# A decoder trunk whose norms apply the token scale after the matmuls, with the keys loaded during the mixers and one engine's one-hots made in two sweeps

## The chip, the cores and the metric

The kernel runs on one core of one Trainium2 chip. A core has five engines that run their own instruction queues and wait for one another through semaphores: PE (matmul; its weight loads are listed apart as PEld), DVE (vector), ACT (scalar), POOL (GpSimd) and SP (which here only issues DMAs). Each engine takes its instructions strictly in the order in which the program lists them, so an instruction that waits holds up all that stands behind it. The metric is the device time of one execution in microseconds (us); lower is better.

## The reference, cut to what matters

256 tokens of width 1024 pass through four residual steps: an attention and retention mixer, a PEER expert step, a short-convolution mixer, and a second PEER step. Before each step stands an RMS norm, and a last one stands at the end:

```python
def rmsnorm(x, g):
    y = xf * lax.rsqrt(jnp.mean(xf * xf, axis=-1, keepdims=True) + EPS)   # one scale per token
    return y * g                                                          # one gain per column

q  = (t @ w_q).reshape(n_tok, 8, 2, 128)            # PEER: queries, 8 heads x 2 halves
sc = einsum('thpd,hpnd->thpn', q, sub_keys)         # scores against 128 keys a half
s1, i1 = top_k(sc[:, :, 0], 16); s2, i2 = top_k(sc[:, :, 1], 16)
# the best 16 of all 256 sums s1+s2 name 16 of 16384 experts a head; softmax over them is the gate
hid = gelu(einsum('td,thkd->thk', t, u[eidx])); out = einsum('thk,thkd->td', gate * hid, v[eidx])

bg, cg, hx = split(xn @ w_in, 3)                    # short convolution
y = conv3(cg * hx);  out = (bg * y) @ w_out
```

The norm's scale is a number per token, its gain a number per column. A scale per token can be taken out of any product that contracts over the columns, and applied to the result.

## The kernel before, in words

The residual `h` lies in SBUF as two halves of 128 tokens by 1024 columns. A matmul with float32 accuracy is built of three: weights are split on the chip into a high part (a cast on ACT, L143) and a low part (a subtraction on DVE or POOL, L145), activations likewise, and high x high, high x low and low x short are added in PSUM. `Stream` loads 512 KB weight blocks in one fixed order into 8 buffers from SP's queue, and splits them a few ahead of their use (`ahead`, `next`).

`Norm` stands between the steps. The mixer's last loop (`v_phase`) ends with four quarters of the output (a half of the tokens by 512 columns); after each, DVE adds it to `h` (L293) and `norm.done(a, ...)` runs. `quarter` squares and sums on ACT (L349), takes the root there (L362), makes the reciprocal with one step of Newton's method on DVE (`rstd`, L368 to L373), multiplies `h` by the gain (L353), and puts the token scales on a diagonal matrix `dg`. `finish` turns `h` to columns by tokens with matmuls against `dg` (L380), which applies the scales on the way, runs 8 dummy matmuls (`busy`, L316), and writes the high, low and short parts of the result: `x2` and `Xb`. For PEER a float32 copy `XF` and a copy by tokens `XG` (96 tokens) are written too. `First`, the norm of the input, has its own form: `some` turns the raw half with the diagonal, and writes high and low parts column block by column block with the gain as a scale (L502 on ACT, L503 on DVE).

`even_mixer` runs 28 weight blocks into four PSUM accumulators, with a table of work to be put between the blocks (`steps`); `rope`, `evac` and others take results out of PSUM. `odd_mixer` runs three blocks a column block, with a short chain on ACT and DVE behind each.

`peer` has three stages. The **score stage**: 16 blocks of `wq`, each a tile of 24 matmuls (`u_tile`, L248 and L261), a copy of the result (L1098), the matmul with the keys (`scores`, L957) and a copy of that out of PSUM (L960). A `Pump` hands the search for the best 16 (L944 to L952) to DVE behind it, which goes on far into the next stage. The keys are loaded into `KO` by POOL at the start of `peer` (L935), after `KO`'s memory, which the mixer's tiles used, is free. The **dense u stage**: 128 blocks of `pu` for the 160 tokens that are not gathered, while 96 tokens have their experts' rows gathered by POOL's indirect DMAs (L837) and multiplied on DVE (L847). Here `onehots` (L1135, L1136) builds on ACT, per token, |iota - index| and then a relu of it, whose products on PE spread the gates over the experts. The **dense v stage** does the same with `pv`.

What sets the order is the program itself: every instruction is listed by hand, and nothing is reordered.

## Time and profile before

| | us |
|---|---|
| median of 3 runs | 1547.38 (1544.8 to 1550.67) |
| the profiled execution, its own time | 1543.23 |
| its span in the trace | 1541.5 |
| PE busy | 1484.1 (96%) |
| DVE busy | 1163.8 (75%) |
| ACT busy | 797.2 (52%) |
| POOL busy | 687.4 (45%) |
| bytes moved | 533.55 MB, a mean of 346 GB/s |

A row of the timeline holds the start in us from the span's start, the length in us, engine and line, the operation, the tile written and the tiles read, and in brackets the idle time before it and what ended it; rows of one line are merged (x16 is 16 instructions). A row of the windows holds the stretch, its length, then for PE, PEld, DVE, ACT and POOL the busy time and the number of instructions, the share of full speed at which PE's clock was granted, the share of the 16 DMA engines in use, and GB/s. Matmuls overlap, so a busy PE is not a PE at its best.

### The profile page before, as it was taken

The numbers are of one execution on the slowest core, as the hardware profiler recorded it, in microseconds if no ns is written. First come the engines' busy times: TensorE is split into PE (matmuls) and PEld (weight loads), VectorE is DVE, ScalarE is ACT, GpSimd is POOL, SyncE is SP. The second block draws the span as 40 slices with busy tenths as digits, with TensorE's granted clock in tenths as the row PEclk, the third lists the DMA queues.
The fourth block names the chain that finished last, engine by engine and source line by source line (L and its number), as shares of the span: only waits on it lengthen the run. The fifth ranks groups of instructions, "written<-read, shape, count | busy, mean of one in ns | idle before, by whom it ended". The sixth has DMA issues, their size and how long they took to land.

```text
span 1541.5 us, 30553 instructions
## 1 busy us (share of the span) xinstructions
PE 1484.1 (96%) x11183; PEld 1392.5 (90%) x11196; DVE 1163.8 (75%) x2514; ACT 797.2 (52%) x1974; POOL 687.4 (45%) x522
## 2 busy tenths in 40 slices
PE   8998999999999899999989989999999999999997
PEld 5666999999999899999989789999999998999996
DVE  3637999957888777777674569997688887777785
ACT  5555412158988244444554353212898954444454
POOL 6653645544654333333047365455455552333310
PEclk9999999999999999999999999999999999999998
DMA  8344889999999999999945477999999999999993
GB/s 316 145 150 165 326 333 408 382 407 406 408 409 408 395 395 406 391 407 403 367 163 194 158 262 293 404 404 370 408 409 408 408 405 394 407 399 400 407 393 130
DMA packets 146998, 533.55 MB, mean 346 GB/s; under 512 B 16928, under 2 KB 17056, under 8 KB 146848
## 3 DMA queue, kind: packets, MB, share of 16 engines
q1 hardware_dynamic: 71568, 258.87, 43.7%
q0 software_dynamic: 56704, 205.07, 34.0%
q10 hardware_dynamic: 18576, 67.64, 11.3%
q8 instruction: 89, 1.46, 0.4%
q14 instruction: 61, 0.50, 0.1%
HBM read 528.85 MB, written 1.05 MB: 344 GB/s over the span
## 4 chain that ended last, share of the span: by engine, by line
PE 41%; DMA 24%; DVE 24%; issue 5%; ACT 4%; POOL 2%; SPq 0%; DVEq 0%; ACTq 0%; POOLq 0%
DMA raw<-pv 10%; PE vo L1268 8%; PE vo L1272 8%; PE hid L1178 6%; DMA rows<-pun,ig 5%; DVE rows L847 4%; PE vo L1274 4%; PE hid L248 4%; DMA grow<-pv,ig 3%; DMA rows<-pv,ig 3%; DVE grow L847 2%; DMA grow<-pun,ig 2%; DVE hg L946 2%; DVE hg L952 2%; DVE hg L948 2%
## 5 line engine op out<-in xcount | busy, mean ns | idle before, releaser
L1178 PE MATMUL hid<-xf,raw 128*128 128x160 f32 x3648 | 520.6, 302 | 13.0 <-DVE hg L1212 7.0
L1178 PEld LDWEIGHTS hid<-xf,raw 128*128 128x128 f32 x3648 | 505.5, 192 | 14.7 <-DVE hg L1212 8.3
L1189 ACT CAST vhi<-raw 128x1024 fp32r<-128x1024 f32 x160 | 167.5, 1047 | 252.2 <-DMA raw<-pv 205.6
L1196 DVE TENSOR_TENSOR vlo<-raw,vhi 128x1024 bf16<-128x1024 f32 x160 | 195.8, 1224 | 119.7 <-ACT vhi L1189 117.9
L837 POOL DMA_INDIRECT rows<-pv,ig x128 | 154.3, 1206 | 260.0 <-DVE gacc L861 206.6
L145 POOL TENSOR_TENSOR lo<-raw,hi 128x1024 bf16<-128x1024 f32 x76 | 182.1, 2408 | 118.6 <-ACT hi L143 106.4
L1272 PE MATMUL vo<-hs,vhi 128*128 128x320 f32 x1280 | 229.1, 321 | 2.0 <-DVE hs L1249 1.7
L1268 PE MATMUL vo<-hg,raw 128*128 128x160 f32 x1536 | 228.9, 302 | 0.6 <-DVE hg L1212 0.6
L837 POOL DMA_INDIRECT rows<-pun,ig x128 | 156.3, 1221 | 135.5 <-DVE rows L847 88.9
L1268 PEld LDWEIGHTS vo<-hg,raw 128*128 128x128 f32 x1536 | 211.6, 190 | 1.1 <-DVE hg L1212 1.1
L1272 PEld LDWEIGHTS vo<-hs,vhi 128*128 128x128 f32 x1280 | 190.6, 188 | 4.9 <-DVE hs L1249 4.3
L847 DVE SCALAR_TENSOR_TENSOR rows<-rows,xg 128x1024 f32<-128x1024 f32 x128 | 155.0, 1220 | 27.4 <-DMA rows<-pun,ig 26.7
L861 DVE SCALAR_TENSOR_TENSOR gacc<-rows,ghid,gacc 128x1024 f32<-128x1024 f32 x124 | 158.7, 1280 | 14.2 <-DMA rows<-pv,ig 13.8
L1209 ACT ACTIVATE hg<-hid 128x160 f32<-128x160 f32 (+25 forms) x242 | 64.1, 269 | 192.7 <-PE hid L1178 188.3
L1136 ACT ACTIVATE ko<-ko,idxT 128x128 f32<-128x128 f32 x320 | 157.9, 493 | 10.6
L837 POOL DMA_INDIRECT grow<-pv,ig x64 | 78.3, 1224 | 121.6 <-DVE gacc L861 91.3
L1135 ACT ACTIVATE ko<-cst,idxT 128x128 f32<-128x128 f32 x320 | 124.1, 388 | 5.5 <-PE G L1145 5.5
L248 PE MATMUL hid<-x,hi 128*128 128x256 f32 x896 | 123.5, 291 | 0.5 <-ACT x L389 0.3
L1274 PE MATMUL vo<-hb,vlo 128*128 128x160 bf16 x1280 | 116.3, 234 | 0.0
L143 ACT CAST hi<-raw 128x1024 fp32r<-128x1024 f32 x100 | 104.1, 1051 | 20.3 <-issue 7.5
L248 PEld LDWEIGHTS hid<-x,hi 128*128 128x128 f32 x896 | 112.8, 195 | 1.4 <-ACT x L389 1.1
L837 POOL DMA_INDIRECT grow<-pun,ig x64 | 77.2, 1206 | 75.0 <-DVE grow L847 45.0
(235 smaller groups left out, 2020.3 us busy)
## 6 DMA issues: line engine op xcount, KB each, us to landing
raw<-pu SPq DMA_DIRECT2D x228, 512.0 KB, 7.6
raw<-pv SPq DMA_DIRECT2D x128, 512.0 KB, 8.3
raw<-pv ACTq DMA_DIRECT2D x128, 512.0 KB, 7.8
raw<-wq SPq DMA_DIRECT2D x32, 512.0 KB, 3.7
raw<-ew_in SPq DMA_DIRECT2D x28, 512.0 KB, 4.3
raw<-ow_in SPq DMA_DIRECT2D x24, 512.0 KB, 4.3
hg<-pu SPq DMA_DIRECT2D x22, 512.0 KB, 5.0
raw<-ew_out SPq DMA_DIRECT2D x8, 512.0 KB, 3.2
```

Of the source, the lines that this page charges most:

```text
L145: eng.tensor_tensor(lo, t, hi.bitcast(F32), OP.subtract)
L248: pe.matmul(ps[:, :S], hi[:, k * P:(k + 1) * P], A2[:, k, s_, :], start=k == 0 and s_ == 0, stop=False)
L837: gp.indirect_dma_start(self.row(s_), None, table, bass.IndirectOffsetOnAxis(IG[:, 0, s_ % STEPS:s_ % STEPS + 1].bitcast(U32), 0))
L847: v.scalar_tensor_tensor(r, r, 1.0, XG[:, q % 2, :], op0=OP.mult, op1=OP.mult, accum_out=w)
L861: v.scalar_tensor_tensor(self.acc[q], r, w, self.acc[q], op0=OP.mult, op1=OP.add)
L1136: act.activation(B[:, j], B[:, j], AF.Relu, bias=idxT[:, 2, t:t + 1], scale=idxT[:, 3, t:t + 1])
L1178: pe.matmul(ps[:, :TD], w[:, k * P:(k + 1) * P], XF[:, k, :], start=k == 0, stop=k == ND - 1)
L1189: act.copy(whi[j], raw)
L1196: v.tensor_tensor(wlo[j], raw, whi[j].bitcast(F32), OP.subtract)
L1268: pe.matmul(vo[b][:, :TD], w[:, b * P:(b + 1) * P], HG[:, i, :], stop=False, **m)
L1272: pe.matmul(vo[b][:, :2 * TD], hi[:, b * P:(b + 1) * P], hs, stop=i == NK - 1, **m)
L1274: pe.matmul(vo[b][:, :TD], lo[:, b * P:(b + 1) * P], hb, stop=i == NK - 1, **m)
```

## The change

Three things. **The norms.** `First` goes, and `Norm` is written anew. After each quarter the raw `h` is turned with plain transposes (`turn`), with no gain and no scale; `parts` writes the high and low parts with the gain as a scale per column, for all norms. The token scale is made later and applied where results leave PSUM: in `rope`, `evac`, `scores`, and in the odd mixer. Where it must lie along the free axis, `spread` makes it so on PE. `rows`, called in the score stage behind the first tile, writes `XF` and `XG`, which `finish` wrote before. The 8 dummy matmuls go; at the start 24 are left of 36. **The keys.** `KO` is now held for the whole kernel, and `load_keys` runs in the mixer before. **The one-hots.** The four first steps of a group come before the four second steps.

```diff
+    KO = pers.tile([P, NPAIR * NK], F32, tag="ko", name="ko")
...
+    class Norm(Sums):
...
+        def turn(self, a):
+            th, ch = a // 2, a % 2
+            if th == 0:
+                for j in range(2):
+                    self.ps[ch, j] = acc_tile(j, nm("xt")) if ch else side_tile(nm("xt"))
+            for k in range(4):
+                kk = ch * 4 + k
+                o = (k % 2 * 2 + th) * P
+                pe.transpose(self.ps[ch, k // 2][:, o:o + P], h[:, th, kk * P:(kk + 1) * P], ident)
+
+        def parts(self, ch):
+            x2 = xv["x2"]
+            for k in range(4):
+                kk = ch * 4 + k
+                ps = self.ps[ch, k // 2][:, k % 2 * S:(k % 2 + 1) * S]
+                gain = G[:, (3 + self.gi) * ND + kk:(3 + self.gi) * ND + kk + 1]
+                act.activation(x2[:, kk, 0, :], ps, AF.Copy, scale=gain)
+                v.scalar_tensor_tensor(x2[:, kk, 1, :], ps, gain, x2[:, kk, 0, :].bitcast(F32),
+                                       op0=OP.mult, op1=OP.subtract)
+                if k % 2:
+                    gp.tensor_copy(Xb[:, kk - 1:kk + 1, :], x2[:, kk - 1:kk + 1, 0, :].bitcast(F32))
+
+        def done(self, a, junk):
+            if a == 1:
+                self.turn(0)
+            if a < 3:
+                self.square(a, junk)
+            if a == 1:
+                self.mean0(0)
+                self.root(0)
+            if a == 2:
+                self.turn(1)
+                self.rstd(0)
+                self.mean0(1)
+            if a == 3:
+                new_x2()
+                self.turn(2)
+                self.parts(0)
+                self.turn(3)
+                self.square(a, junk)
+                self.parts(1)
+                self.root(1)
+                st.ahead(0)
+                self.rstd(1)
+
+        def first(self, junk):
+            new_x2()
+            for a in (0, 2, 1, 3):
+                self.turn(a)
+            self.parts(0)
+            st._split()
+            st._split()
+            self.parts(1)
+            for a in range(4):
+                self.square(a, junk)
+            for th in range(2):
+                self.mean0(th)
+                self.root(th)
+                self.rstd(th)
+            st.ahead(0)
+
+        def spread(self):
+            for th in range(2):
+                v.tensor_scalar(self.wb[:, th], ident, 0.0, self.scale(th), op0=OP.mult, op1=OP.add)
+            ps = side_tile(nm("rb"))
+            for th in range(2):
+                pe.matmul(ps[:, th * P:(th + 1) * P], self.wb[:, th], ident, start=True, stop=True)
+            return ps[:, :S]
+
+        def rows(self):
+            ps = self.spread()
+            x2 = xv["x2"]
+            v.tensor_tensor(XF, x2[:, :, 0, TG:].bitcast(F32), x2[:, :, 1, TG:].bitcast(F32), OP.add)
+            v.tensor_tensor(XF, XF, ps[:, None, TG:].to_broadcast([P, ND, TD]), OP.mult)
+            v.scalar_tensor_tensor(XG[:TG, 0, :], h[:TG, 0, :], self.scale(0)[:TG], XG[:TG, 1, :],
+                                   op0=OP.mult, op1=OP.mult)
+            act.copy(XG[:TG, 1, :], XG[:TG, 0, :])
+            for q in range(2):
+                gp.dma_start(XG[TG:, q, :], XG[q * SUB:(q + 1) * SUB, 0, :])
...
+    def load_keys(l):
+        for c in (slice(0, 4 * NK), slice(4 * NK, NPAIR * NK)):
+            gp.dma_start(KO[:, c], keys[l][:, c])
...
-                    v.tensor_tensor(a, a, co[:, None, :].to_broadcast([P, NH, HD]), OP.mult)
+                    times(a, a, co, HD)
...
-            at(0, rest)
+            at(14, lambda: load_keys(0))
...
                 ps = u_tile(xv["x2"], Xb, first=k == 0)
+                if k == 0:
+                    rb = before.spread()
+                    act.copy(rs[:, 0], rb)
+                    v.tensor_tensor(rs[:, 1], rb, rs[:, 0], OP.mult)
+                    load_keys(1)
                 cg = mp2.tile([P, S], F32, tag="cg", name=nm("cg"))
-                act.copy(cg, ps[:, :S])
+                v.tensor_tensor(cg, ps[:, :S], rs[:, 1], OP.mult)
...
                 v.tensor_tensor(z, ps[:, :S], y, OP.mult)
+                v.tensor_tensor(z, z, rs[:, 0], OP.mult)
...
-                    act.copy(sc(th, f), ps[:, th * NK:(th + 1) * NK])
+                    act.activation(sc(th, f), ps[:, th * NK:(th + 1) * NK], AF.Copy, scale=before.scale(th))
...
                 act.copy(qT[f % 2], ps[:, :S])
+                if f == 0:
+                    before.rows()
...
                     act.activation(B[:, j], iota, AF.Abs, bias=idxT[:, 1, t:t + 1], scale=-1.0)
+                for j in range(GT):
+                    t = g * GT + j
                     act.activation(B[:, j], B[:, j], AF.Relu, bias=idxT[:, 2, t:t + 1], scale=idxT[:, 3, t:t + 1])
...
-        busy(36)
-        norm.start(acc_tile(3, nm("junk")))
+        busy(24)
+        norms[0].first(acc_tile(3, nm("junk")))
```

In the last norm (`Final`) the two token factors are multiplied once in `rstd`, ahead of all four output pieces; before, they were two operands, and only the piece on ACT needed the product (L522).

More of the change, by code (lines that the diff above doesn't have):

```diff
@@ L403, in short @@
-        def short(self, th, half, eng):
-            k, t = self.at(th, half)
-            (act.copy if eng is act else eng.tensor_copy)(Xb[:, k, t], xv["x2"][:, k, 0, t].bitcast(F32))
-        def quarter(self, a, junk):
+            v.scalar_tensor_tensor(w[5], w[1], 1.0 / D, w[2], op0=OP.mult, op1=OP.add)
+            v.reciprocal(w[4], w[3])
+            v.scalar_tensor_tensor(w[6], w[4], w[5], w[4], op0=OP.mult, op1=OP.mult)
+            v.tensor_scalar(w[6], w[6], -0.5, 1.5, op0=OP.mult, op1=OP.add)
@@ L506, in trunk_kernel @@
-    class Final(Norm):
-        def done(self, a, junk):
-            self.quarter(a, junk)
-            if a == 3:
                 for ch in range(2):
                     self.put(0, ch, v)
-                run(self.rstd(1)[:-2])
+                self.rstd(1)
                 for ch in range(2):
@@ L768, in even_mixer, with odd_mixer @@
             v_phase(ND, part, each, norm.done)
[L770 removed]
+    def odd_mixer(before, norm):
         with tc.tile_pool(name=nm("mix"), bufs=1) as mp, tc.tile_pool(name=nm("mix2"), bufs=2) as mp2:
```

219 lines of the change are left out of this document (60 added, 159 removed).

## The prediction

> **What bounds the kernel now.** First the head of the page, then the stretches, to see which stage has which limit.
>
> ```profile
> span 1541.5 us, 30553 instructions
> ```
>
> ```profile
> 30.00:116.00 86.00, 85.86 (x422) 54.79 (x428) 37.15 (x90) 44.00 (x73) 54.26 (x27) 1.00 0.43 157
> 250.00:310.00 60.00, 57.04 (x420) 56.79 (x419) 58.74 (x190) 10.44 (x30) 33.21 (x28) 1.00 1.01 390
> 370.00:430.00 60.00, 59.11 (x455) 58.90 (x454) 49.74 (x104) 57.31 (x180) 35.30 (x28) 1.00 1.02 407
> ```
>
> In the mixer (30 to 116) PE is full and the DMA share is 0.43; in a dense stage (370 to 430) the DMAs are full, at 1.02 and 407 GB/s. Between them lies a stretch in which DVE is the full engine (250 to 310: 58.74 of 60): it works off the search for the best 16 that the score stage, 137 to 193, hands it. So in the norms and mixers each us on PE's path counts, in the score stage the moment from which DVE has work without a break, and in the dense stages bytes.
>
> Second, the timeline of the seam between the mixer and the first score stage, and the group of the key matmuls.
>
> ```profile
> 120.25 0.38 PE L694 MATMUL rt<-cst,ro 128*128 128x128 f32 x2
> 131.62 0.39 PE L273 MATMUL acc<-lo,cbe 128*128 128x512 bf16 x1
> 139.67 1.05 PE L261 MATMUL hid<-xb,lo 128*128 128x256 bf16 x8
> 140.48 2.15 PE L248 MATMUL hid<-x,hi 128*128 128x256 f32 x16
> 142.40 1.29 POOL L935 DMA_DIRECT2D ko<-keys  x2 [6.62 <-ACT xg L454]
> 147.02 0.68 PE L957 MATMUL sc<-ko,hg 128*128 128x128 f32 x4 [3.50 <-issue]
> 147.74 0.43 ACT L960 COPY hg<-sc 128x128 f32<-128x128 f32 x2 [3.25 <-PE sc L957]
> 149.04 0.28 DVE L944 MAX8 hg<-hg 128x8 f32<-128x128 f32 x1
> 152.81 0.29 DVE L944 MAX8 hg<-hg 128x8 f32<-128x128 f32 x1 [0.28 <-ACT hg L960]
> ```
>
> ```profile
> L957 PE MATMUL sc<-ko,hg 128*128 128x128 f32 x128 | 20.2, 282 | 7.7 <-DMA ko<-keys 4.2 <-issue 3.5
> ```
>
> The mixer's last matmul ends at 132.0 (131.62 + 0.39), the first query tile at 140.7, and a tile takes 2.8 us (140.48 to 143.3). Then PE stands still for 3.50 us until the keys, asked for at 142.40, have come; in the second score stage for 4.2. DVE begins at 149.04 and waits 0.28 at 152.81; the timeline of DVE alone shows no further wait up to 200.
>
> The stall costs more than itself. By the us, PE's granted clock falls:
>
> ```profile
> 147.00:148.00 1.00, 0.98 (x8) 1.00 (x9) 1.00 (x1) 0.26 (x2) 1.00 (x1) 0.91 1.03 260
> 150.00:151.00 1.00, 1.00 (x7) 0.85 (x6) 0.93 (x5) 0.00 (x0) 1.00 (x1) 0.50 0.91 340
> 151.00:152.00 1.00, 1.00 (x10) 0.88 (x9) 0.90 (x6) 0.00 (x0) 0.56 (x1) 0.88 0.84 299
> ```
>
> From 147.8 to 151.2 PE runs at half speed, 3.4 us, which loses 1.7. In the second score stage the stall costs more:
>
> ```profile
> 888.76 2.15 PE L248 MATMUL hid<-x,hi 128*128 128x256 f32 x16
> 896.02 1.20 PE L957 MATMUL sc<-ko,hg 128*128 128x128 f32 x4 [4.22 <-DMA ko<-keys]
> 903.11 0.29 DVE L944 MAX8 hg<-hg 128x8 f32<-128x128 f32 x1 [2.00 <-ACT hg L960]
> ```
>
> Both stages run the same instructions, 748.3 us apart (second tiles: 888.76 and 140.48). So 903.11 is 154.8 on the first stage's scale, 2.0 later than 152.8.
>
> **The change, part by part, on the first stage's scale.** The keys now arrive before the stage, in a mixer whose DMAs stand at 0.43. POOL spends 1.3 us on it (row 142.40), some blocks ahead of use: nothing. That takes away 3.50 + 1.7 and, in the second stage, 4.2 and its slow tile. What is late next decides.
>
> The new norm is not shorter. `parts` has the order of `First`, whose rows show its pace:
>
> ```profile
> 10.07 0.47 ACT L502 ACTIVATE x<-xt,small 128x256 fp32r<-128x256 f32 x1
> 11.10 0.84 ACT L502 ACTIVATE x<-xt,small 128x256 fp32r<-128x256 f32 x2 [0.55 <-DVE x L503]
> 12.52 0.47 ACT L502 ACTIVATE x<-xt,small 128x256 fp32r<-128x256 f32 x1 [0.58 <-DVE x L503]
> ```
>
> ACT and DVE take turns on a PSUM tile (ACT waits for DVE's L503): four column blocks take ACT from 10.07 to 12.99, and DVE's last low part 0.45 more: 3.4 us, eight 6.8. The turns put ahead of the last quarters add 8 transposes to PE, 0.07 each by the spacing behind row 120.25: 0.5. Last matmul 132.6; the last quarter is added by DVE until 133.3; `parts(0)` begins when `turn(2)` is through, 133.1, with its first low part held to 133.5 by that addition; the last square sits on ACT ahead of `parts(1)`:
>
> ```profile
> 131.38 0.60 ACT L349 ACTIVATE acc<-h 128x512 f32<-128x512 f32 x1 [0.34 <-DVE h L293]
> 131.92 0.19 ACT L349 ACTIVATION_READ_ACCUMULATOR acc<-h 128x1 f32 x1
> 133.77 0.29 ACT L362 ACTIVATE nw<-nw 128x1 f32<-128x1 f32 x1
> 134.16 0.15 DVE L368 SCALAR_TENSOR_TENSOR nw<-nw 128x1 f32<-128x1 f32 x1
> 134.87 0.42 DVE L372 TENSOR_SCALAR dg<-cst,nw 128x128 f32<-128x128 f32 x1
> 139.02 1.05 ACT L143 CAST hi<-raw 128x1024 fp32r<-128x1024 f32 x1
> 140.10 1.23 DVE L145 TENSOR_TENSOR lo<-raw,hi 128x1024 bf16<-128x1024 f32 x1 [1.29 <-ACT hi L143]
> 140.92 1.16 ACT L454 ACTIVATE xg<-xs,nw 96x1024 f32<-96x1024 f32 x1
> ```
>
> With 0.75 for it and its sum, the last high part comes at 139.6 and the last low part at 140.1. Eight high x low matmuls (1.07) and eight short ones (1.05) remain: the first tile ends at 142.0, 1.3 later than before.
>
> Now the new wait. `rows` puts two matmuls (`spread`) behind the first tile in PE's queue, and the second tile stands behind them. They need the scales spread by DVE. ACT, after the last high part: root 0.29, two casts of 1.05, ending at 140.9 and 142.0. DVE's queue in the changed program: low part of the second block until 142.2 (it waits for the first cast, then 1.23), five small operations of `rstd` (0.7 from 134.16 to 134.87 for four, 0.9 with the fifth), low part of the third block 143.1 to 144.3, two spreads (0.35 apart, somewhat under the like-shaped L372), 145.0. So PE waits from 142.0 to about 145.0: 3.0 to 3.3 us in place of the keys' 3.5. The second tile ends at 148.1, the third at 151.2; before, with the slow clock, the third ended at 152.0. PE is 0.6 early at full clock, 1.5 late if this stall too halves the clock.
>
> DVE pays more. `rows` then gives it 1280, 1280 and 1024 elements a row; 1.23 for 1024 makes 1.5 + 1.5 + 1.2, until 149.2. Behind it ACT copies `XG` (1.16, 150.4) and only then casts the fourth block (151.5), copies the second tile's result and the first scores (some 0.4 each, row 147.74): the search begins at 152.3 instead of 149.04, and its second group, 3.4 later, at 155.7 instead of 152.8. **So +2.9 for DVE in the first stage, +0.9 in the second (against 154.8).** The value lies between PE's shift and DVE's, nearer to DVE's, which is full until 310: +2.0, bounds -0.6 and +2.9; second stage +0.4, bounds -2.6 (PE's -0.6 and the 2.0 by which this stage ran later before) and +0.9.
>
> The seam before the odd mixer has no keys to gain:
>
> ```profile
> 779.13 2.82 PE L1289 MATMUL fq<-cst,xg 128*128 128x128 f32 x16 [1.05 <-DVE xg L1284]
> 786.00:787.00 1.00, 1.00 (x7) 1.00 (x6) 0.89 (x6) 0.58 (x1) 0.24 (x1) 0.56 0.00 0
> 794.29 2.15 PE L248 MATMUL hid<-x,hi 128*128 128x256 f32 x16
> ```
>
> Here DVE adds the quarters without PE between them, and in the new order `rstd` and the second mean come ahead of the last addition: by the same sums `parts` ends at 791.2, the first tile at 793.0, but the spreads, behind two low parts, at 795.4, and the second tile starts at 795.8 instead of 794.29: +1.5, and with some half clock (from 786.1 on before as well, row 786) +2.0, bounds 0 and +4. The rest of that mixer gives DVE two short operations a column block, beside 8.4 us of matmuls: nothing.
>
> The start:
>
> ```profile
> 5.50 0.60 ACT L349 ACTIVATE junk<-h 128x512 f32<-128x512 f32 x1 [2.82 <-DMA h<-x]
> 26.23 0.59 PE L271 MATMUL ea<-hi,x 128*128 128x512 f32 x1
> ```
>
> Before, the input is there at 5.5 and the second accumulator group starts at 26.23. In the new order the turns end `parts(0)` at 10.0 (ACT 9.5) instead of 13.5, but ACT then has two casts (to 11.5), `parts(1)` with a wait for a low part on DVE (14.3), four squares and two roots (17.6) and only then the third block's cast, 18.6; DVE, behind the second `rstd`, ends its low part at 20.6. Twenty-two matmuls of 512 columns (0.23, twice 2.8 / 24) make 25.8 for the group, or 27.5 if PE's idle time from 7 to 10.5 costs clock: +0.3, bounds -0.5 and +2.
>
> One-hots:
>
> ```profile
> 401.14 0.39 ACT L1135 ACTIVATE ko<-cst,idxT 128x128 f32<-128x128 f32 x1
> 401.56 0.49 ACT L1136 ACTIVATE ko<-ko,idxT 128x128 f32<-128x128 f32 x1
> 401.96 0.38 ACT L1135 ACTIVATE ko<-cst,idxT 128x128 f32<-128x128 f32 x1
> ```
>
> A second step starts 0.42 after its first, a next first step 0.40 after that, 0.09 ahead of the end. Independent neighbours would overlap by 0.09 each time: some 0.3 of 3.3 us a group, 12 us of ACT a layer. ACT is nearly full there (57.31 of 60), but so are the DMAs; the bytes remain. Nothing; at most -6 in all, should PE's waits there shrink.
>
> The end:
>
> ```profile
> 1537.24 0.15 DVE L522 TENSOR_TENSOR nw<-nw 128x1 f32<-128x1 f32 x1
> ```
>
> The last piece waited for L522 behind the other; it now starts some 0.6 earlier, and the diagonal's 0.3 goes: -0.9. The scales in `rope`, `evac` and `scores` replace operations of the same size: nothing.
>
> Sum: +0.3 + 2.0 + 2.0 + 0.4 - 0.9 = **+3.8 us**. Against the profiled execution, 1543.2 (span 1541.5 and 1.7 around it), that is 1547.0; that execution was 4.2 below the median of the runs shown, so for a median I say **1551**.
>
> **Rivals.** *The clock* (the slower side). In 133 to 140 PE now has one short matmul in 0.85 us, a share of 0.16, where before the diagonal and dummy matmuls filled it, and then the new stall. In the rows above, the stretch from 144.4 to 147.8, of which PE worked in 0.8 us, was followed by 3.4 us at half clock. If every seam loses one or two such stretches, each 1.7, that is +5 to +8 on top: 1557 to 1560. [...] *The keys' stall goes and nothing takes its place*: if the scales are ready by 142, the third tile ends at 147.9 instead of 152.0, -4.1, and in the second stage 2.0 more, -6.1; with the start, the odd seam and the end that is 1547.4 + 0.3 + 2.0 - 0.9 - 10.2 = 1539. Against it stands the order of DVE's queue. *ACT's relief counts*: 1551 - 6 = 1545; against it the DMAs at 1.02. *The two sweeps save no ACT time at all*: 1551, as forecast.
>
> **How the numbers follow.** Forecast (sum between -2 and +9) 0.54, clock 0.24, keys 0.16, ACT 0.06. 0.5% is 7.7 us, about what a measurement can tell from no change: under 1539.6 is faster, over 1555.1 slower. Faster: the keys, 0.16. Slower: the clock and the forecast's top (0.04 of it), 0.28. Same: 0.50 of the forecast and ACT's, 0.56. Range: from just above the keys' time, 1540, to the clock's top, 1560.
>
> **What would show it.** In the changed trace: the key matmuls without a wait for `ko`; the spread matmuls (`rb`) with 3 us of idle PE before them, ended by DVE; the first search at about 152 and 900.5; half clock behind the seams; the one-hots' second steps 0.4 apart and the DMAs still at 1.02. If the spread's wait is under 1 us, the forecast is wrong to the fast side; if half clock lasts over 7 us at a seam, to the slow side.

## The result, and the profile after

The changed kernel takes 1559.09 us (median of 10 runs, 1555.52 to 1565.55) against 1546.42 (10 runs) for the kernel before: ratio 1.0082, 95% interval 1.0066 to 1.0099. It is slower by 12.7 us. The time lies in the range of the prediction (1540 to 1560), but not where the likeliest case stood (1551, no difference); slower had a chance of 0.28. The profiled execution took 1556.92, its span is 13.5 longer than before:

```profile
span 1555.0 us, 30407 instructions
```

Where the 13.5 come from is read from the same marks in both timelines: the first quarter that DVE adds at the end of the even mixer, the mixer's last matmul, the first dense matmul (its moving operand is `xf`), the dense stage's last matmul, the second query tile of the odd mixer, and so on. Timeline of the kernel before (start, duration, engine, line), as far as the prediction has not shown it:

```profile
127.87 0.69 DVE L293 TENSOR_TENSOR h<-acc,h 128x512 f32<-128x512 f32 x1 [3.10 <-PE acc L273]
194.43 0.84 PE L1178 MATMUL hid<-xf,hg 128*128 128x160 f32 x5
777.35 0.73 PE L1274 MATMUL vo<-hb,vlo 128*128 128x160 bf16 x8
879.91 0.39 PE L273 MATMUL acc<-lo,cbo 128*128 128x512 bf16 x1
944.74 0.44 PE L1178 MATMUL hid<-xf,hg 128*128 128x160 f32 x2
1527.30 0.73 PE L1274 MATMUL vo<-hb,vlo 128*128 128x160 bf16 x8
```

and of the changed kernel:

```profile
132.65 0.69 DVE L294 TENSOR_TENSOR h<-acc,h 128x512 f32<-128x512 f32 x1 [3.07 <-PE acc L274]
137.28 0.39 PE L274 MATMUL acc<-lo,cbe 128*128 128x512 bf16 x1
199.98 1.25 PE L1162 MATMUL hid<-xf,hg 128*128 128x160 f32 x8
783.53 0.73 PE L1255 MATMUL vo<-hb,vlo 128*128 128x160 bf16 x8
806.28 3.17 PE L249 MATMUL hid<-x,hi 128*128 128x256 f32 x16
894.48 0.39 PE L274 MATMUL acc<-lo,cbo 128*128 128x512 bf16 x1
957.43 0.84 PE L1162 MATMUL hid<-xf,hg 128*128 128x160 f32 x5
1541.18 0.73 PE L1255 MATMUL vo<-hb,vlo 128*128 128x160 bf16 x8
```

| mark (an end is start plus duration) | before | after | behind by | this stretch |
|---|---|---|---|---|
| first quarter added, even mixer | 127.9 | 132.7 | +4.8 | start +4.8 |
| mixer's last matmul ends | 132.0 | 137.7 | +5.7 | turns between the last matmuls +0.9 |
| first dense matmul, layer 1 | 194.4 | 200.0 | +5.6 | score stage -0.1 |
| dense stage's last matmul ends | 778.1 | 784.3 | +6.2 | +0.6 |
| second query tile, odd mixer | 794.3 | 806.3 | +12.0 | odd seam +5.8 |
| mixer's last matmul ends | 880.3 | 894.9 | +14.6 | odd mixer +2.6 |
| first dense matmul, layer 2 | 944.7 | 957.4 | +12.7 | score stage -1.9 |
| dense stage's last matmul ends | 1528.0 | 1541.9 | +13.9 | +1.2 |
| span | 1541.5 | 1555.0 | +13.5 | end -0.4 |

The loss sits at the start and at the odd seam; the score stages, where the keys' stall was, gain little. At the start (timeline of PE, and the stretch 8 to 30 with busy times of PE, PEld, DVE, ACT, POOL, then granted clock and DMA share):

```profile
11.21 0.50 PE L272 MATMUL ea<-hi,x 128*128 128x512 f32 x1 [2.85 <-ACT hi L143]
17.84 1.65 PE L272 MATMUL ea<-hi,x 128*128 128x512 f32 x3 [6.13 <-ACT junk L333]
8.00:30.00 22.00, 12.80 (x46) 7.38 (x45) 7.88 (x22) 14.01 (x25) 13.55 (x9) 0.77 0.74 287
```

After its first matmul PE stands still for 6.13, until ACT's last square (L333) has written its scrap, `junk`. That tile is `acc_tile(3)`, which is also one of the two accumulators of the first group; the second matmul wants it. Before, the squares came first, and no matmul waited for them. The clock is lower as well: 0.77 on average over this stretch, 1.00 before.

In the first score stage, timeline and clock by stretch (in the stretches the first figure is PE's busy time, the third last the granted clock):

```profile
148.90 1.20 PE L443 MATMUL rb<-cst,nwb 128*128 128x128 f32 x4 [0.57 <-DVE nwb L440]
153.16 1.04 ACT L454 COPY xg<-xg 96x1024 f32<-96x1024 f32 x1 [4.42 <-DVE xg L452]
155.72 0.29 DVE L924 MAX8 hg<-hg 128x8 f32<-128x128 f32 x1 [2.59 <-ACT hg L940]
137.00:143.00 6.00, 3.50 (x17) 1.95 (x16) 3.60 (x10) 3.71 (x11) 1.32 (x3) 1.00 0.00 0
143.00:153.00 10.00, 8.96 (x38) 7.63 (x39) 8.62 (x15) 3.11 (x6) 1.13 (x2) 0.50 0.29 106
```

The spread waits 0.57 for DVE, not 3; but the clock is half from 143 to 153, behind a stretch in which PE worked 3.50 of 6 us. The key matmuls wait for nothing any more, by their group (busy, mean ns of one, idle time before):

```profile
L937 PE MATMUL sc<-ko,hg 128*128 128x128 f32 x128 | 19.5, 275 | 0.0
```

The odd seam:

```profile
799.75 1.93 PE L262 MATMUL hid<-xb,lo 128*128 128x256 bf16 x8
801.78 1.22 DVE L145 TENSOR_TENSOR lo<-raw,hi 128x1024 bf16<-128x1024 f32 x1 [1.59 <-ACT hi L143]
802.11 3.09 POOL L145 TENSOR_TENSOR lo<-raw,hi 128x1024 bf16<-128x1024 f32 x1 [3.82 <-ACT hi L143]
802.92 2.56 DVE L440 TENSOR_SCALAR nwb<-cst,nw 128x128 f32<-128x128 f32 x2
805.43 1.20 PE L443 MATMUL rb<-cst,nwb 128*128 128x128 f32 x4 [3.75 <-DVE nwb L440]
```

Here the first tile ends at 801.68, its short matmuls at half clock (1.93 instead of 1.05); the spread's wait is 3.75, the two diagonals (L440) take 2.56, and the first of them ends 0.1 behind GpSimd's low part, 802.11 to 805.20. The group of L440 by duration (least, median, most, in ns) says that it is one instruction:

```profile
L440 DVE TENSOR_SCALAR nwb<-cst,nw x6: 275/278/2361, 148.5 to 905.9; 128x128 f32<-128x128 f32 x6
```

The one-hots are as forecast: the second steps of a group start 0.39 apart (402.50, 402.89, 403.27, 403.66), and the DMAs still stand at 1.03 from 375 to 435. The page's busy times:

```profile
PE 1488.8 (96%) x11095; PEld 1389.4 (89%) x11108; DVE 1174.9 (76%) x2534; ACT 767.3 (49%) x1972; POOL 672.8 (43%) x522
```

ACT is busy for 767 us instead of 797, and the dense stages are no shorter.

If all that the mean granted clock (0.989 of 1541.5 us before, 0.982 of 1555.0 after) lacks of 1.00 is time at 0.50, as in the stretch from 143 to 153, PE ran at half speed for some 34 us before and 56 after. At half speed a us loses at most 0.5; by this estimate the clock can account for at most 11 of the 13.5, and for less where PE waited anyway.

### The profile page after: what moved, and what is told of

It is laid out like the page before. It is cut to its first block, busy times and chain, and to the rows that moved or that the text cites. A ratio compares the mean times of both kernels' runs of the same rounds, so it can differ in the third digit from the quotient of the medians.

```text
span 1555.0 us, 30407 instructions
## 1 busy us (share of the span) xinstructions
PE 1488.8 (96%) x11095; PEld 1389.4 (89%) x11108; DVE 1174.9 (76%) x2534; ACT 767.3 (49%) x1972; POOL 672.8 (43%) x522
## 3 DMA queue, kind: packets, MB, share of 16 engines
HBM read 528.34 MB, written 1.05 MB: 340 GB/s over the span
## 4 chain that ended last, share of the span: by engine, by line
PE 33%; DMA 31%; DVE 23%; issue 6%; ACT 4%; POOL 2%; ACTq 0%; DVEq 0%; POOLq 0%
DMA raw<-pv 16%; DMA rows<-pun,ig 9%; PE vo L1249 6%; DMA grow<-pv,ig 5%; PE vo L1253 5%; PE hid L1162 5%; DVE rows L833 3%; PE hid L249 3%; PE vo L1255 2%; PE ea L272 2%; DVE hg L926 2%; DVE hg L932 2%; DVE hg L928 2%; DVE grow L833 2%; PE ea L273 2%
## 5 line engine op out<-in xcount | busy, mean ns | idle before, releaser
L1162 PE MATMUL hid<-xf,raw 128*128 128x160 f32 x3648 | 517.3, 300 | 14.9 <-DVE hg L1196 8.6
L823 POOL DMA_INDIRECT rows<-pv,ig x128 | 150.4, 1175 | 271.7 <-DVE gacc L847 216.7
L823 POOL DMA_INDIRECT rows<-pun,ig x128 | 151.3, 1182 | 139.0 <-DVE rows L833 87.3
L847 DVE SCALAR_TENSOR_TENSOR gacc<-rows,ghid,gacc 128x1024 f32<-128x1024 f32 x124 | 158.6, 1279 | 16.2 <-DMA rows<-pv,ig 15.7
L249 PE MATMUL hid<-x,hi 128*128 128x256 f32 x896 | 133.3, 301 | 8.1 <-ACT x L390 8.1
L1120 ACT ACTIVATE ko<-ko,idxT 128x128 f32<-128x128 f32 x320 | 130.8, 481 | 0.0
L249 PEld LDWEIGHTS hid<-x,hi 128*128 128x128 f32 x896 | 119.0, 201 | 12.5 <-ACT x L390 12.0
L1117 ACT ACTIVATE ko<-cst,idxT 128x128 f32<-128x128 f32 x320 | 101.6, 390 | 22.4 <-PE G L1129 22.3
```

The lines of the kernel that those rows point to most:

```text
L249: pe.matmul(ps[:, :S], hi[:, k * P:(k + 1) * P], A2[:, k, s_, :], start=k == 0 and s_ == 0, stop=False)
L823: gp.indirect_dma_start(self.row(s_), None, table, bass.IndirectOffsetOnAxis(IG[:, 0, s_ % STEPS:s_ % STEPS + 1].bitcast(U32), 0))
L847: v.scalar_tensor_tensor(self.acc[q], r, w, self.acc[q], op0=OP.mult, op1=OP.add)
L1120: act.activation(B[:, j], B[:, j], AF.Relu, bias=idxT[:, 2, t:t + 1], scale=idxT[:, 3, t:t + 1])
L1162: pe.matmul(ps[:, :TD], w[:, k * P:(k + 1) * P], XF[:, k, :], start=k == 0, stop=k == ND - 1)
```

## The experiments

Two theories: **the clock** (PE is sparse at the seams, runs at half clock, and that is the price) and **the chain** (the price is the order of work on DVE and ACT: low part, scale, diagonals, row operations, copy of `XG`, cast, in front of what PE and the search wait for). For the start, the accumulator against the clock. Line numbers differ by a few between these kernels. Each ratio is to the kernel before as it ran beside that kernel (medians of 1546.3 to 1547.4). The marks, worked out from the timelines as above; "search" and "dense" are the first search and the first dense matmul, counted from the end of the mixer's last matmul, layer 1 and 2; "odd seam" is from the end of the first dense stage to the second query tile:

| kernel | first quarter | search | dense | odd seam | time us (runs) | ratio to before, 95% |
|---|---|---|---|---|---|---|
| before | 127.9 | 17.0, 17.3 | 62.4, 64.4 | 16.2 | 1546.4 (10) | |
| changed | 132.7 | 18.1, 18.1 | 62.3, 62.6 | 22.0 | 1559.1 (10) | 1.0082 (1.0066 to 1.0099) |
| scrap elsewhere | 129.2 | 18.1, 18.1 | 60.5, 60.5 | 21.1 | 1555.4 (5) | 1.0062 (1.0042 to 1.0082) |
| dummy matmuls | 134.4 | 18.1, 18.1 | 60.5, 60.5 | 19.0 | 1553.1 (10) | 1.0041 (1.0018 to 1.0063) |
| diagonals early | 131.3 | 17.4, 17.4 | 59.9, 59.9 | 17.7 | 1552.1 (10) | 1.0038 (1.0026 to 1.0051) |
| dummies, copy on GpSimd | 132.5 | 15.6, 15.9 | 60.3, 60.7 | 19.0 | 1554.0 (5) | 1.0056 (1.0037 to 1.0076) |
| all four | 129.0 | 14.8, 14.9 | 59.6, 59.8 | 15.4 | 1546.2 (10) | 0.9991 (0.9972 to 1.0010) |
| one sweep | 132.9 | 18.1, 18.1 | 62.1, 60.5 | 21.1 | 1560.3 (10) | 1.0076 (1.0055 to 1.0097) |
| keys late again | 134.0 | 18.1, 18.1 | 62.0, 62.5 | 20.9 | 1558.5 (1) | |
| before, keys alone | 128.2 | 12.8, 12.8 | 57.2, 57.3 | 16.1 | 1541.4 (10) | 0.9954 (0.9941 to 0.9967) |
| blocks in another order | 131.8 | 16.0, 16.0 | 59.7, 59.8 | 18.3 | 1549.7 (1) | |
| before, keys alone, by SP | 127.8 | 12.7, 12.7 | 57.2, 57.2 | 15.9 | 1534.1 (6) | 0.9916 (0.9898 to 0.9933) |
| all that helped | 128.0 | 12.9, 13.0 | 57.7, 57.9 | 13.3 | 1540.9 (7) | 0.9953 (0.9935 to 0.9970) |
| fifth low part on DVE | 133.0 | 18.1, 18.1 | 62.1, 60.5 | 19.7 | 1566.9 (1) | |

A dense stage, from its first matmul to its last, takes between 581.7 and 593.6 in these executions, in no order that follows the edits (585.0 to 589.7 in the two kernels that are the one before with other key loads); why is open. Single times are therefore not compared here, only marks, and medians of several runs.

**Scrap elsewhere.**

```diff
-        norms[0].first(acc_tile(3, nm("junk")))
+        norms[0].first(hid_tile(nm("junk")))
```

> The squares at the start write their scrap into the hid tile that the dummy matmuls had, not into the fourth accumulator. The accumulator theory (PE's second matmul waits 6.13 us for the scrap tile to come free): the first two blocks' matmuls follow the high parts from 11.2 on, the third block's cast (19.17) sets the rest, and the first quarter is added at 127.4 to 128.4 instead of 132.65; all later marks move by the same 4.3 to 5.2, the time by -5. The rival, the clock (PE stands idle from 8.4 to 11.2 and runs at half clock until 23.7 whatever it waits for): the group then loses some 2 us to the clock anyway, the mark comes at 130 to 131, and the time moves by -2.

```profile
11.16 2.07 PE L272 MATMUL ea<-hi,x 128*128 128x512 f32 x4 [2.85 <-ACT hi L143]
129.24 0.69 DVE L294 TENSOR_TENSOR h<-acc,h 128x512 f32<-128x512 f32 x1 [3.07 <-PE acc L274]
```

The wait of 6.13 is gone and the mark comes at 129.24. The changed kernel's own start, run seven times with this code (the changed kernel and six experiments that leave it alone), gives 131.3 to 134.4, mean 133.0: so the accumulator is worth 3.7, between the two forecasts. Some half clock stays (0.84 over 8 to 30), as the rival had it. The time's gain of 3.7 fits, though its interval overlaps that of the changed kernel. The dense marks fell too, to 60.5, with no edit there: in this execution the half clock lay earlier in the first seam (0.72 from 139 to 143, then 0.90 to 149; in the changed kernel 1.00 to 143, then 0.50), over the sparse part. Four executions leave the score seams as the change made them, eight score stages in all: four have 62.1 to 62.6 at this mark, four 60.5. The mark goes with the place of the half clock, which none of these edits sets: in the changed kernel's two stages (62.3 and 62.6) and the first with the fifth low part on DVE (62.1) the second tile's 16 long matmuls take 3.69, 3.76 and 3.49; in the second stages of that kernel and of one sweep (60.5 both) they take 2.15.

**Dummy matmuls.**

```diff
                 for k in range(ND):
+                    if s_ == 0 and k:
+                        fill(4)
                     one(k, s_)
...
             ps = side_tile(nm("rb"))
+            fill(12)
```

`fill(n)` issues n matmuls of the zero tile `Z` into `acc_tile(2)`, like `busy`.

> At the three seams PE gets dummy matmuls: four between the first eight matmuls of the first tile, twelve ahead of the spread matmuls. The clock theory (the seams' loss is half clock): the half clock after the first tile goes at all three, the first search comes some 2.2 us earlier in both score stages (155.72 to 153.5, 912.93 to 910.7 less what came before), the second tile of the odd mixer 2 us earlier, the time by -6. The chain theory (the loss is the queue low part, scales, spread, three row operations on DVE, then the copy of XG and a cast on ACT, in front of the copies that the search waits for): the clock is full again, but the first search stays within 0.4 of 18.05 us behind the mixer's last matmul, PE waits 2 us for the spread instead, and only the odd seam gains, 1.5 to 2; the time moves by -2.

The mixer's last matmul, the end of the first tile, the spread, the first search, and the clock behind the first tile:

```profile
139.06 0.39 PE L276 MATMUL acc<-lo,cbe 128*128 128x512 bf16 x1
147.26 1.05 PE L264 MATMUL hid<-xb,lo 128*128 128x256 bf16 x8
150.59 0.71 PE L451 MATMUL rb<-cst,nwb 128*128 128x128 f32 x4 [0.97 <-DVE nwb L447]
157.50 0.29 DVE L932 MAX8 hg<-hg 128x8 f32<-128x128 f32 x1 [2.59 <-ACT hg L948]
145.00:155.00 10.00, 9.03 (x77) 8.07 (x76) 8.53 (x15) 2.96 (x6) 0.91 (x2) 1.00 0.32 107
```

The clock is 1.00 where it was 0.50, and the first search stays 18.05 behind the last matmul, to the hundredth: the chain theory's mark. But PE's own path gained: the first dense matmul comes 1.8 and 2.1 earlier, the odd seam is 3.0 shorter, the odd mixer behind it 1.0. Half clock is a real price, 6.0 of the 12.7 between medians of ten runs, on PE's path and not on DVE's. At the dense marks the dummies make sure of the 60.5 that the unmended seam has in four stages of eight. The diagonal that takes 2.36 stays (L447 there: 274/277/2360, least, median and most in ns) while the clock is 1.00 from 797 to 811, so that delay is not the clock's. Neither theory alone had all of it.

**Diagonals early.**

```diff
                 self.root(1)
-                st.ahead(0)
                 self.rstd(1)
+                self.wide()
+                st.ahead(0)
```

`wide` holds the two diagonals, which `spread` then finds made.

> The second half's scale and both spreads' diagonals are made by DVE right behind the last root, ahead of the weights' low parts; nothing else changes. The chain theory: in the odd seam the diagonals are there at 799.9 instead of 805.5 and take 0.47 instead of 2.56, since no low part of GpSimd runs beside them; the spread follows the first tile at once and the second tile starts at 801.8 instead of 806.28; -4.5 there, at most -0.5 in the score stages, the time -4 to -5. The clock theory: the second tile starts earlier, but at half clock, which gives some of it back: -2 to -2.5 in all.

```profile
L440 DVE TENSOR_SCALAR nwb<-cst,nw x6: 278/279/282, 144.3 to 900.1; 128x128 f32<-128x128 f32 x6
803.03 2.15 PE L249 MATMUL hid<-x,hi 128*128 128x256 f32 x16
```

The odd seam falls from 22.0 to 17.7, no diagonal takes longer than 0.282, the time falls by 7, more than the 4 to 5 told. The chain theory's mark (17.5) for the odd seam, and a little more in the score stages than its 0.5 allowed (2.4 and 2.7 at the dense mark; the place of the half clock has part in that, since moving the scrap alone gave 1.8 and 2.1 there).

**Dummies, copy on GpSimd.** The dummies, and

```diff
-            act.copy(XG[:TG, 1, :], XG[:TG, 0, :])
+            gp.tensor_copy(XG[:TG, 1, :], XG[:TG, 0, :])
```

> The dummy matmuls of the other kernel, and GpSimd instead of ACT copies the gained rows within XG. The chain theory: now neither PE's second tile nor ACT's copy holds the first scores, and the first search comes 1.5 to 2.5 us earlier than with the dummies alone, in both score stages; the time is 3 to 5 below that kernel. The clock theory: ACT's copy was never what the search waited for, and this kernel equals the one with the dummies alone within 0.5 at both marks.

The search moves as the chain theory said, by 2.5 and 2.2. The time does not: 1554.0 against 1553.1, and the first dense matmul comes at 60.3 and 60.7 instead of 60.5. So what the search waits for is not what the dense stage waits for. DVE's earlier start buys nothing as long as PE reaches the dense stage at the same moment: that part of the expectation, 3 to 5 of time, fell.

**All four.** The edits above in one kernel, with `fill(4)` ahead of the spread.

> All four edits in one kernel: the scrap in the hid tile, the dummy matmuls (four each, also ahead of the spread), the diagonals ahead of the low parts, the copy of XG on GpSimd. The seams theory (what the changed kernel lost, it lost at the start and the three seams, and the gains add on PE's path): mixer's last matmul at about 134.3, first search 15 behind it, first dense matmul 58.5 to 60 behind it, 15.5 instead of 22.0 from the first stage's end to the second query tile of the odd mixer, and a time of 1543 to 1546, no slower than the kernel before. The rival (the dense stages themselves have become longer, 584.3 to 589.6 in the changed kernels against 583.3 and 583.7 before): the marks come as told, but each dense stage takes 586 or more and the time is 1548 to 1551.

The marks come as the seams theory told (134.05, 14.8, 59.6, 15.4) and the ratio is 0.9991: no net loss is left. That doesn't mean that these places held all of it: against the kernel before, the start is still 1.2 longer, the turns cost 0.9 in each mixer, and the odd mixer is 3.1 longer, and the score stages, 2.8 and 4.7 shorter, pay for it. One cause in the odd mixer is a new operation that was put at nothing, `z` times the scale on DVE:

```profile
802.88 3.22 DVE L791 TENSOR_TENSOR z<-z,rs 128x256 f32<-128x256 f32 x1
809.23 2.15 PE L249 MATMUL hid<-x,hi 128*128 128x256 f32 x16 [1.26 <-DVE cg L781]
```

It takes 3.22 instead of 0.42 beside two low parts of GpSimd's (801.10 to 805.81), and PE waits 1.26 for what stands behind it on DVE. The time of 1546.2 is at the upper edge of the forecast. The dense stages took 587.6 and 587.2 in the profiled execution, as the rival had it, but its time (1548 to 1551) did not come, and dense stages as long stand in kernels with the old norm too.

**One sweep.** `Abs` and `Relu` next to each other again in `onehots`.

> The changed kernel with the one-hots' two steps next to each other again, token by token, as before the change. The bytes theory (the dense stages are set by the DMAs, ACT's relief buys nothing and costs nothing): ACT's busy time returns from 767 to about 797, both dense stages stay within the spread of single executions (583 to 590), and the time is that of the changed kernel within 2. The rival (two sweeps make a dense stage longer): both dense stages fall to 583.5 and the time by 3 to 6. The other rival (ACT's relief did help): the time rises by 3 to 6.

```profile
PE 1493.8 (95%) x11095; PEld 1393.4 (89%) x11108; DVE 1172.2 (75%) x2534; ACT 799.1 (51%) x1972; POOL 681.8 (44%) x522
```

ACT is busy for 32 us more and the time is the same (1.0076 against 1.0082, the intervals lie on each other). The dense stages of the profiled execution, 593.6 and 589.4, are not within the 583 to 590 that was expected, but that execution (1568.9) lies 8.6 above its kernel's median. Two sweeps relieve ACT and buy nothing.

**Keys late again.** `load_keys(l)` in front of the first query tile, in both layers.

> The changed kernel with the keys asked for in front of the first query tile again, in both score stages. The hidden theory (in the changed kernel something later than the keys holds the first scores anyway): GpSimd asks for them at some 145, they land 4.6 later at 149.6, the first key matmul comes at 154 without a wait, and the first search stays 18.05 behind the mixer's last matmul: nothing changes, so the early load bought nothing here. The rival (the stall of the kernel before comes back): 3 us or more of idle PE ahead of the key matmuls ended by ko, and the first search 2 to 3.5 later.

```profile
146.24 1.29 POOL L541 DMA_DIRECT2D ko<-keys  x2
155.24 0.61 PE L935 MATMUL sc<-ko,hg 128*128 128x128 f32 x4
157.09 0.30 DVE L922 MAX8 hg<-hg 128x8 f32<-128x128 f32 x1 [2.59 <-ACT hg L938]
```

No wait ahead of the key matmuls, and the search 18.07 behind the last matmul: in the changed kernel the early keys are worth nothing, because the new norm reaches the first scores later than the keys do. The first dense matmul says the same, 62.0 and 62.5 against 62.3 and 62.6.

**Before, keys alone.** The kernel before, without `KO` and its loads in `peer`, and with

```diff
+    KO = pers.tile([P, NPAIR * NK], F32, tag="ko", name="ko")
...
+            at(14, lambda: load_keys(0))
...
-            norm = Norm(mp, gi)
+            norm = Norm(mp, gi, xs=XG)
...
+                if k == 0:
+                    load_keys(1)
```

> The kernel before with the keys alone loaded during the mixers (the mixers' norms keep their gained rows in XG to make room), and no other part of the change. If the keys' stall stands on PE's path with nothing behind it, the key matmuls follow the second tile at once, the first search comes at 145 to 146 instead of 149.04, the half clock behind the stall goes, the first dense matmul comes some 5 earlier in the first stage and 6 in the second, and the time is 1536 to 1540. If another wait stands behind it (the copies on ACT, DVE's row operations), the searches move by under 1 and the time by under 2. If the dense stages take the gain back, the marks move, and the time does not.

```profile
145.05 0.30 DVE L949 MAX8 hg<-hg 128x8 f32<-128x128 f32 x1 [0.48 <-ACT hg L965]
```

In the old norm the same step is worth 5.9 us (0.9954), to a time just above the forecast: the search comes 4.3 and 4.5 earlier, the dense matmul 5.2 and 7.2. It would be more, but the odd mixer loses 4.5 (90.6 from its second tile to its last matmul instead of 86.0). There, timeline:

```profile
801.32 6.07 DVE L145 TENSOR_TENSOR lo<-raw,hi 128x1024 bf16<-128x1024 f32 x1
801.62 4.68 POOL L145 TENSOR_TENSOR lo<-raw,hi 128x1024 bf16<-128x1024 f32 x2
807.78 2.50 PE L249 MATMUL hid<-x,hi 128*128 128x256 f32 x14 [2.69 <-DVE u L793]
```

A low part that takes DVE 1.22 alone takes 6.07 beside a cast and two low parts of GpSimd's: it ends at 807.39, 1.09 behind them (801.06 to 806.30). PE waits 2.69 for what stands behind it on DVE. GpSimd's request for the keys, 1.14 from 795.20 on, stands ahead of these low parts in its queue.

**Blocks in another order.**

```diff
-            for k in range(4):
+            for k in (0, 2, 1, 3):
```

in `parts`, and the same order in the first tile.

> The changed kernel with the eight column blocks of a norm in the order 0, 2, 1, 3, 4, 6, 5, 7 (also in the first tile), so that ACT's block and DVE's block lie in different PSUM tiles. The turn theory (ACT waits 0.55 and DVE 0.5 because both read one PSUM tile in turn): the waits of 0.5 go, the eight blocks take ACT 4.3 to 4.8 from first to last with the square between them, instead of 6.32 (137.93 to 144.25), and the first search comes 1.5 to 2 earlier, at 16 to 16.5 behind the mixer's last matmul. The rival (the waits are latency between the engines, whatever tile): the pace and the 18.05 stay.

```profile
137.12 0.84 ACT L390 ACTIVATE x<-xt,small 128x256 fp32r<-128x256 f32 x2 [0.60 <-PE xt L381]
138.15 0.87 ACT L390 ACTIVATE x<-xt,small 128x256 fp32r<-128x256 f32 x2 [0.19 <-DVE x L391]
139.53 0.83 ACT L390 ACTIVATE x<-xt,small 128x256 fp32r<-128x256 f32 x2
140.54 0.87 ACT L390 ACTIVATE x<-xt,small 128x256 fp32r<-128x256 f32 x2 [0.19 <-DVE x L391]
```

The waits of 0.55 go; 0.19 stays each time ACT comes back to a tile. The eight blocks take 4.29 (137.12 to 141.41) instead of 6.32, the search comes at 16.0. The waits were for the tile, not for the other engine. Whether the tile's memory or the program's own order between the readers of a tile sets them, the trace doesn't say.

**Before, keys alone, by SP.**

```diff
-                if k == 0:
-                    load_keys(1)
+                if k == 4:
+                    load_keys(1, nc.sync)
```

> The kernel before with the keys alone, as tried, but the second layer's keys asked for by SP at the fifth column block of the odd mixer instead of by GpSimd at the first. The collision theory (GpSimd's request pushed its low parts into DVE's, which then took 6.07 for one low part, stopped PE for 2.69 and halved the clock): from the second query tile to the odd mixer's last matmul 86 to 87 instead of 90.56, the score stages stay at 12.75, and the time is 1536 to 1538. The rival (the keys' bytes delay that mixer wherever they are asked for): 89 to 91 there, and 1540 to 1542.

The odd mixer is back at 86.0 (790.18 to 876.19), the score stages as in the kernel with the keys alone, and the ratio is 0.9916: 13.3 us below the kernel before, better than both kernels of the comparison and than the forecast of 1536 to 1538. The marks add up to 12.7 of it. The edit moves the request to another engine and also to a later block; which of the two did it, this run doesn't separate. In the stretch where the kernel before had stood still (PE busy for 0.00 of the 3 us from 144 to 147) and then run at half clock (0.50 from 148 to 151):

```profile
144.00:147.00 3.00, 3.00 (x29) 2.88 (x28) 2.27 (x12) 1.83 (x6) 2.85 (x3) 1.00 0.86 255
148.00:151.00 3.00, 3.00 (x28) 2.88 (x27) 2.79 (x15) 1.52 (x5) 3.00 (x2) 1.00 1.02 381
```

**All that helped.** The four edits (dummies two and four), the other order of blocks, the keys by SP.

> The changed kernel with all that helped: scrap in the hid tile, diagonals early, copy of XG on GpSimd, blocks in the order 0, 2, 1, 3, dummy matmuls (two a block, four ahead of the spread), the second layer's keys by SP at the fifth column block. The seams theory: the norm on two PSUM tiles saves 2 at the start and at each seam more than the four edits did: first dense matmul 57 to 58 behind the mixer's last, 13.5 to 14 from the first stage's end to the second odd tile, time 1536 to 1540, level with the kernel before plus early keys. The rival (scales at the ends cost DVE and PE as much as the diagonals did, whatever the order): 59 or more in the score stages and a time of 1543 to 1547.

The marks came as told (57.7 and 57.9; 13.3), the time of 1540.9 is just above the forecast. Against the old norm with early keys by SP, the new norm, mended, is 2.6 better at the odd seam and 0.5 and 0.6 worse at the score stages; it pays 0.9 for the turns in each mixer, and the odd mixer takes 88.1 instead of 86.0. So it ends behind: by the marks outside the dense stages the two differ by some 1.6 us, by time by 6.8, and the dense stages make 2.6 of that in the profiled executions. The rest is open.

**Fifth low part on DVE.**

```diff
-    srcs += [(ow_in[f], i not in (1, 2) and i % 4 != 3) for i, f in enumerate(OF)]
+    srcs += [(ow_in[f], i not in (1, 2, 4) and i % 4 != 3) for i, f in enumerate(OF)]
```

> The changed kernel with one flag turned: the low part of the odd mixer's fifth weight block (802.11 to 805.20 on GpSimd in the changed kernel's trace) is made by DVE, ahead of the spread's diagonals. The collision theory (one diagonal took 2.36 instead of 0.28 because GpSimd's low part ran beside it): with GpSimd idle all six diagonals take 0.28; DVE has 1.2 more ahead of them, so they end at 21.0 less 0.8 behind the first stage's end, and the spread comes 0.5 to 1 earlier although more work stands in front of it. The rival (the diagonal is slow for another reason, such as the half clock or the keys' request): one of the six still takes 2.3, and the spread comes 1.2 later.

```profile
L440 DVE TENSOR_SCALAR nwb<-cst,nw x6: 279/282/282, 148.8 to 912.0; 128x128 f32<-128x128 f32 x6
811.94 3.65 PE L249 MATMUL hid<-x,hi 128*128 128x256 f32 x16
```

With GpSimd idle beside them all six diagonals take 0.28, and the second tile comes 19.7 behind the dense stage instead of 22.0 (20.9 to 22.0 in the four other executions in which this seam is as the change made it), with 1.2 more work of DVE ahead of it. With the clock full and GpSimd busy the slow diagonal stayed (dummy matmuls), with GpSimd idle it goes: the collision is shown. Its single time, 1566.9, goes with dense stages of 592.1 and 590.6 and says nothing on the edit.

## Why the prediction was right and wrong, step by step

- **Start, +0.3 (bounds -0.5 and +2): +4.8. Failed.** The order of ACT's work was right (`parts` at the pace told, the third cast at 19.17 against 18.6), but "the squares" were costed as time on ACT and not as holders of a tile: the scrap tile is an accumulator of the first group. Without that wait the start costs +1.2 to +1.4 (129.02 and 129.24 against 127.87), inside the bounds: a wait for a tile was put at nothing.
- **First score stage, +2.0 (-0.6 to +2.9): +0.8 with the turns.** The chain on DVE and ACT was right in kind and 1.6 too long: the search was expected 19.7 behind the last matmul (152.3 less 132.6) and came at 18.05. Choosing the value near DVE's shift was the mistake: the copy on GpSimd moved the search by 2.5 and the time by nothing. PE's arrival at the dense stage is what counts. "3 us of idle PE" ahead of the spread was 0.57, because half clock let the first tile end 1.8 later (10.7 behind the mixer's last matmul, 8.9 with the dummies); with the clock full the gap from the tile's end (148.31) to the spread (150.59) is 2.3. The turns ahead of the mixer's end were put at 0.5 and took 0.9. The line "if the wait is under 1 us the forecast is wrong to the fast side" was wrong: a wait can also be short because PE is late.
- **Odd seam, +2.0 (0 to +4): +5.8. Failed by size.** The order was right, spreads behind two low parts. Counted from the dense stage's end, which came 6.2 later than before, the diagonals were to end at 801.6 and ended at 805.48: 2.1 of it is the collision with GpSimd's low part, which the sum didn't have. The rest goes with the first tile, which ended at 801.68 where the sum had 799.2, at half clock (0.50 from 795 to 801): DVE's second low part, which stands ahead of the diagonals, starts at 801.78, 0.1 behind the tile's end. With the clock full (dummy matmuls) the diagonals end 18.7 behind the dense stage instead of 21.2. The dummies alone give 3.0 back, the early diagonals 4.4, the kernel with both 6.7.
- **The rest of the odd mixer, nothing: +1.7** (+2.6 with the turns' 0.9, which the next line counts). 1.0 goes with the dummies: the second tile's 16 long matmuls take 3.17 without them (granted clock 0.74 from 801 to 809) and 2.15 with them (1.00 from 803 to 811); 0.7 is open. The two short operations on DVE were not free either once the seam was mended: one of them cost PE 1.26 beside GpSimd's low parts.
- **Second score stage, +0.4 (-2.6 to +0.9): -1.0 with the turns.** Right.
- **Keys, a stall with the scales next behind it: right**, and shown from both sides: late keys cost the changed kernel nothing, early keys alone give the old one 5.9, and 13.3 when SP asks for the second layer's, later.
- **One-hots, nothing: right**, ACT's 30 us included (24 were worked out). **The end, -0.9: -0.4.**
- **The clock rival** (0.24, 1557 to 1560) is the case that came: half clock for ten us at a seam, and 6 by time when it is taken away, within the 5 to 8 it was given. Its sign came too, half clock for over 7 us at a seam. PE's share in the sparse stretch was put at 0.16; from 139.60 to 143.00 it was 0.44 (1.50 of 3.40), and the clock fell all the same. That the time lies where this rival had it, and inside the range, is in part luck, since the prediction knew neither the scrap's wait nor the collision, while the score stages gave less loss than the sum had. PE's share of a stretch does not give the clock in that stretch: at the odd seam of the changed kernel PE was busy for 3.41 of 3.41, with transposes alone (L381, L1270), at 0.50, and right behind it for 1.99 of 3.38 at 1.00:

```profile
788.10:791.51 3.41, 3.41 (x18) 3.16 (x16) 2.33 (x9) 2.05 (x8) 0.00 (x0) 0.50 0.10 37
791.52:794.90 3.38, 1.99 (x9) 1.14 (x8) 1.86 (x5) 2.25 (x7) 1.22 (x2) 1.00 0.00 0
```

## What to carry to other kernels

When work is moved on an engine, list the tiles it holds as well as the time it takes: a scrap output in a tile that is wanted next turns a free reordering into a stall. Before a stall is removed, ask what stands next in line; here the same early load was worth nothing beside one norm and 0.5% beside the other, 0.8% once an engine without work of its own asked for it, and later. At a seam of an engine that is full elsewhere, follow that engine's own arrival at the next stage, not the first moment at which another engine has work.

## What the runs showed of the hardware that was not expected

- **Some operations of DVE lasted until GpSimd's beside them were over, and the delay shows as their own length.** A diagonal of 0.28 took 2.36 and ended 0.1 behind a low part of GpSimd's (802.11 to 805.20); with GpSimd idle it took 0.28 again. A low part of 1.22 took 6.07 and ended 1.09 behind three of GpSimd's instructions in a row (a cast and two low parts, 801.06 to 806.30). Others were not delayed: in the kernel before, all 16 of the search's first `MAX8` (L944, 128 columns) that lay inside an operation of GpSimd's took 0.27 or 0.28. What sets the two kinds apart, no run here shows.
- **The start is not the same length twice.** Seven executions of one start gave 131.3 to 134.4 for the first quarter. The mean granted clock from 8 to 30 was 0.77 in the earliest and 0.61 in the latest. That is 3.5 us of full clock less (0.16 of 22), and the marks lie 3.1 apart; but three others with 0.77 gave 132.5 to 132.9, so the mean clock is not all of it. Why the clock differs from execution to execution is not shown.
- **The clock fell without a long gap.** Ahead of the half clock at 143 (0.50 to 153) no gap of PE's from 137.3 on was longer than 0.67, and PE worked 3.50 of the 6 us; with four dummy matmuls in each gap PE worked 5.32 of the 6 us from 139 to 145, and the clock stayed at 1.00.
- **Two engines on one PSUM tile waited 0.55 a block in turns, on two tiles 0.1** (0.19 for every second block), by nothing but the order of the blocks.
